# Gates of two branches as seven quarter products for eight, in a stage of their own ahead of retention

## The chip, the cores and the metric

The kernel runs on one core of a Trainium2 chip. The metric is the device time of one execution in microseconds. The core has a matrix engine (TensorE, PE in the profile; its weight loads are PEld), VectorE (DVE), ScalarE (ACT), GpSimd (POOL) and a sync engine (SP) that issues most of the DMAs. Each engine works through its own instructions in the order in which they were written out, and waits where an operand isn't there.

## The reference

Two blocks follow each other on x of 1024 tokens x 1024 columns, all in fp32. The change touches the first, a layer with four attention branches (a: NSA, b: banded, c: stick-breaking, d: retention) whose results are gated and summed:

```
h = rms_norm(x, norm_g) * (1.0 + scale) + shift
...
branches = ((y_a, a_z), (y_b, b_z), (y_c, c_z), (y_d, d_z))
for i, (y, z) in enumerate(branches):
    yi = y.reshape(B, S, BRANCH_W) * jax.nn.silu(z)
    term = jax.nn.sigmoid(h @ w_merge[i]) * (yi @ w_br[i])
    merged = term if merged is None else merged + term
return x + gate * (merged @ w_out)
```

w_merge[i] is 1024 x 1024, w_br[i] 256 x 1024. The second block (a mixer with attention, convolutions and pooling, then a feed-forward part) follows and is untouched.

## The kernel before

An fp32 product is made of three matmuls of rounded parts: each operand is split into a high part (`copy`, on ScalarE, VectorE or GpSimd) and the rest (`sub_lo`, line 157 on VectorE or 155 on GpSimd), and `mm3` (lines 229 to 231) adds high x high, high x rest and rest x high into one PSUM bank. `hT` holds h transposed and split: 8 chunks of 128 columns for each of two token halves. A gate of 128 columns and one half takes 8 x 3 = 24 matmuls of 128x512 (`gemm_T`); all gates of a branch take 8 x 2 x 24 = 384. With w_br it is 2 x 3 = 6 for each of the 16 pieces.

The branches run in the order d, a, c, b. `branch_d` projects q and k for both halves, then v, and runs retention in eight chunks. `branch_a` (its tile in `tile_of`) runs 16 tiles: two pairs of heads, eight tiles of 128 tokens each. A tile opens with the scores of the compressed keys (lines 1034 and 1035), goes on with scores of selected and window keys (s banks, lines 797 and 799), softmax on VectorE and ScalarE (lines 838 to 860), transposes of P through t banks (line 276), their split (`PT`, lines 147 and 157) and the products with v into an o bank (lines 816 and 1066).

Between those steps `fill` puts filler work, matmuls into mm banks, at places that the tables FD, FA, FB, FC give by (pair, tile): `q` a projection, `g` one group of `pre`, `m` one group of `merge`, `z` a gate of y. `pre` computes gates of 256 columns ahead and stores tanh of them to `pre_d` in DRAM, for the branches and groups of PREO (branches 0, 2, 1; six groups get used). `merge(bi, y, step)` makes four groups of 256 columns: where `pre_d` has no gate it loads w_merge and makes it, 96 matmuls; then 24 matmuls with w_br; then (1 + tanh) x product on VectorE (line 1147 for step 0, 1149 for others) and an addition to the stored sum on GpSimd (line 1150). merge(3) belongs to branch d and runs inside branch a (`mmm` at tile 3, `m` at tile 7 of the first pair). merge(1) runs last, after branch b, and its sums go split into `gT`, which the product with w_out reads.

The program is handed to a list scheduler, which writes each engine's order by priorities and estimated durations; so a piece that is shorter or sits elsewhere also moves what follows it. Matmuls of a bank wait until the bank's last reader is done; weights go through nine `w` slots and blocks of 4 KB a partition through 31 `blk` slots.

In the second block's feed-forward part the same scheme of quarter products as in the change is in use: `product` (lines 1674 to 1676) adds 12 matmuls of a quarter product into a bank, and banks are read and added to again.

Of the kernel before, what the change touches and what calls it, by code (L numbers as in the profile page):

```python
# [17 lines left out]
P = 128  # L18
# [9 lines left out]
_T = dict(STA='s', XN1=0, PWT=1, PO='0x1', PO2={}, PS=2, PSX=0, PSE='a', PB=99, PEA=(0, 1, 4), WB=8, XL=3, CLO='v', STE=None, STW=None, ST1='b', ST2='b', PLP='pvv', WLO2='v', QXP=1, LW='vp', LEAD=10, FD={0: 'g', 1: 'b', 6: 'g'}, FW=(0, 2), AG=0, PREO=(0, 2, 1), PMB=0, PWB=1, PM=3, SG=2, FA={(0, 2): 'g', (0, 3): 'mmm', (0, 7): 'qm', (1, 0): 'gg', (1, 6): 'gz'}, FB={(0, 3): 'm', (0, 7): 'qm', (1, 3): 'm', (1, 5): 'z', (1, 7): 'm'}, FC={(0, 3): 'mm', (0, 7): 'q', (1, 3): 'zm', (1, 6): 'm'}, NORM='v', NORM2='v', CS=4, CSB=8, MM=2, SB=2, TB=3, OB=1, WHI='aaav', WLO='pv', PTH='a', NW=9, NBLK=31, PTB=2, XN=1, AS=(2, 4, 6, 7), CPP=2, CALT=1, WORK='s0 A A A A A A A A p s1 q t c B c B c B c B c 0a 1a P w 5 4 6 7 g 2 3a e u c B e c B c e B c c e B 1b 0b 3b', KS=(2, 0, 3, 1))  # L28
# [48 lines left out]
def hybrid_then_mix_kernel(ctx: ExitStack, tc, I, c1, c2, out, dbg=None, upto=99):  # L77
# [306 lines left out]
    def x_norm(half):  # L384
# [9 lines left out]
        for kp in range(4):  # L394
            xT[half, kp] = blk(F32, (P, 2, 512))
            if half:
                hT.alloc(half, kp)
            for j in range(2):
# [234 lines left out]


# [20 lines left out]
    def branch_d():  # L655
        qT, kT = [blk(), blk()], [blk(), blk()]
        for half in range(2):
            if half:
                if not _T["XN1"]:
                    x_norm(1)  # L660
                start.close()
                cur[0] = att1.enter_context(tc.tile_pool(name="att1", bufs=1))
                if _T["AG"] == 0:
                    ada_gate()
            cs = slice(half * 512, (half + 1) * 512)
            for q in range(4):
# [3 lines left out]
                if q < 2:  # L670
                    copy(qT[q][:, cs], b[:], "a", QS)
                else:
                    copy(kT[q - 2][:, cs], b[:], "v")
        w = load_w([(w_in[:, :, 3212:3468], 0), (w_in[:, :, 640:652], 256)], 268, per=2)
# [4 lines left out]
        ve.tensor_scalar(g2, g2, 0.5, 0.5, op0=ALU.mult, op1=ALU.add)  # L679
        const_group(2176, ("dm", "xi", "zeta"))  # L680
        if _T["AG"] == 1:
            ada_gate()
# [477 lines left out]

    gate = main.tile([P, 8, 12], F32, name="agate", tag="agate", bufs=1)
# [27 lines left out]
    merge(1, yb, 3)  # L1189
    fill(4)  # L1190
# [475 lines left out]
    def chunks(hi, lo):  # L1666

        return lambda k: (hi[k // 2][:, k % 2, :], lo[k // 2][:, k % 2, :])
# [435 lines left out]
```

## Time and profile before

| | us |
|---|---|
| median of 3 runs (lowest, highest) | 2337.06 (2331.92, 2338.48) |
| the profiled execution, its span | 2339.66, 2337.8 |
| TensorE busy, 11004 matmuls | 2239.1 (96%) |
| VectorE busy | 1519.8 (65%) |
| ScalarE busy | 963.0 (41%) |
| GpSimd busy | 491.1 (21%) |
| granted TensorE clock, mean | 0.988 |

The times lie 6.6 us apart, 0.28%. Busy time of an engine is the time in which at least one of its instructions runs. Matmuls overlap, so their durations add up to more than the time they take; spacing of starts is what one costs. A stretch is read by comparing the busy times of the engines in it with its length.

### The profile page before, as it was taken

The page shows a single profiled execution, that of the slowest core. Times are in us where ns is not written, and L with a number is a line of the kernel's source. Part 1 is how long each engine was busy: PE and PEld are TensorE (multiplying, and loading weights), DVE is VectorE, ACT ScalarE, POOL GpSimd, SP SyncE. Part 2 cuts the span into 40 slices and gives each one's busy share as a digit, 9 for nine tenths or more (in the row PEclk, how much of TensorE's full clock was granted, in tenths as well). Part 3 has the DMA queues.
Part 4 walks back from the last instruction along what each step waited for, and adds up shares of the span by engine and source line. Part 5 has one row for each costly group of instructions (what it writes and reads, how often), then busy time and mean ns, then how long its engine had stood idle before and what let it go on. Part 6 is the DMA issues. An engine that isn't in the chain of part 4 may idle for free.

```text
span 2337.8 us, 30294 instructions
## 1 busy us (share of the span) xinstructions
PE 2239.1 (96%) x11004; PEld 1854.8 (79%) x11004; DVE 1519.8 (65%) x2952; ACT 963.0 (41%) x1937; POOL 491.1 (21%) x411
## 2 busy tenths in 40 slices
PE   8999999999988999999998998999999999999898
PEld 6788888888877778877887876777888878888787
DVE  7634456665677865634479777756666776677773
ACT  6211344444545544422322344534544453344442
POOL 4222100010265622234320000012143430000021
PEclk9999999999999999999999999999999999999999
DMA  9421221122132343224221210156556595534222
GB/s 326 156 92 62 59 68 55 46 86 68 41 102 79 109 132 94 83 80 153 90 73 36 64 59 28 56 179 205 169 182 191 194 360 193 173 108 157 94 75 90
DMA packets 202783, 272.72 MB, mean 117 GB/s; under 512 B 17086, under 2 KB 126214, under 8 KB 202634
## 3 DMA queue, kind: packets, MB, share of 16 engines
q1 hardware_dynamic: 194240, 257.95, 34.1%
q10 hardware_dynamic: 8394, 12.84, 1.7%
q8 instruction: 87, 1.43, 0.3%
q14 instruction: 62, 0.51, 0.1%
HBM read 199.43 MB, written 71.32 MB: 116 GB/s over the span
## 4 chain that ended last, share of the span: by engine, by line
PE 46%; DVE 6%; DMA 2%; ACT 1%; issue 1%; POOL 0%; SPq 0%; DVEq 0%; POOLq 0%; ACTq 0%
PE mm L230 6%; PE mm L231 6%; PE mm L229 6%; DVE blk L1334 2%; PE s L1674 2%; PE s L1676 2%; PE s L1675 2%; PE t L276 1%; PE t L2014 1%; PE t L2015 1%; PE t L2016 1%; PE s L2015 1%; PE mm L2015 1%; PE s L2016 1%; PE mm L2016 1%; PE t L1674 1%
## 5 line engine op out<-in xcount | busy, mean ns | idle before, releaser
L229 PE MATMUL mm<-blk,wh 128*128 128x512 f32 x1264 | 505.1, 400 | 16.3 <-DVE tz L1149 7.0
L230 PE MATMUL mm<-blk,wh 128*128 128x512 f32 x1264 | 501.1, 396 | 0.9 <-DVE blk L157 0.9
L231 PE MATMUL mm<-blk,wl 128*128 128x512 f32 x1264 | 499.9, 396 | 1.9 <-POOL wl L155 1.5
L229 PEld LDWEIGHTS mm<-blk,wh 128*128 128x128 f32 x1264 | 238.6, 189 | 68.5 <-DVE tz L1149 9.8
L231 PEld LDWEIGHTS mm<-blk,wl 128*128 128x128 f32 x1264 | 238.6, 189 | 52.0 <-POOL wl L155 1.9
L230 PEld LDWEIGHTS mm<-blk,wh 128*128 128x128 f32 x1264 | 238.7, 189 | 47.5 <-DVE blk L157 1.3
L155 POOL TENSOR_TENSOR wl<-wr,wh 128x1024 fp32r<-128x1024 f32 (+1 forms) x50 | 122.6, 2453 | 479.7 <-ACT wh L147 281.3
L229 PE MATMUL mm<-wh,blk 128*128 128x512 f32 (+3 forms) x544 | 197.3, 364 | 6.2 <-DVE wh L149 1.8
L231 PE MATMUL mm<-wh,blk 128*128 128x512 f32 (+3 forms) x544 | 194.9, 360 | 1.0 <-DVE blk L157 1.0
L157 DVE SCALAR_TENSOR_TENSOR wh<-blk,wh 128x1024 fp32r<-128x1024 f32 x116 | 138.5, 1222 | 72.0 <-issue 56.4
L147 ACT ACTIVATE wh<-blk 128x1024 fp32r<-128x1024 f32 x116 | 116.9, 1053 | 163.1 <-PE s L2015 77.2
L230 PE MATMUL mm<-wl,blk 128*128 128x512 f32 (+3 forms) x480 | 171.1, 357 | 9.5 <-DVE wl L157 9.1
L147 ACT ACTIVATE blk<-mm 64x512 fp32r<-64x512 f32 (+3 forms) x138 | 77.9, 570 | 172.6 <-PE mm L231 112.6
L147 ACT ACTIVATE PT<-t 128x512 fp32r<-128x512 f32 (+3 forms) x224 | 96.0, 460 | 117.4 <-PE o L816 65.0
L157 DVE SCALAR_TENSOR_TENSOR PT<-t,PT 128x512 fp32r<-128x512 f32 (+3 forms) x224 | 110.9, 515 | 38.0 <-ACT PT L147 37.2
L147 ACT ACTIVATE wh<-wr 128x1024 fp32r<-128x1024 f32 (+2 forms) x91 | 93.7, 1031 | 99.4 <-DMA wr<-in_w_in_dram 22.5
L309 POOL TENSOR_TENSOR sm<-sm,mhalf 128x1 f32<-128x1 f32 x64 | 38.0, 597 | 444.3 <-DVE sm L308 428.6
L229 PEld LDWEIGHTS mm<-wh,blk 128*128 128x128 f32 x544 | 104.1, 192 | 24.5 <-DVE wh L149 2.6
L231 PEld LDWEIGHTS mm<-wh,blk 128*128 128x128 f32 x544 | 104.1, 192 | 16.9 <-DVE blk L157 1.8
L230 PEld LDWEIGHTS mm<-wl,blk 128*128 128x128 f32 x480 | 92.3, 192 | 24.2 <-DVE wl L157 11.3
L157 DVE SCALAR_TENSOR_TENSOR wl<-wr,wh 128x1024 fp32r<-128x1024 f32 (+2 forms) x69 | 88.2, 1279 | 30.8 <-PE mm L230 14.0
L1150 POOL TENSOR_TENSOR acc<-tz,acc 128x512 f32<-128x512 f32 x48 | 68.8, 1436 | 132.0 <-DVE tz L1149 91.4
(364 smaller groups left out, 4857.1 us busy)
## 6 DMA issues: line engine op xcount, KB each, us to landing
acc<-acc SPq DMA_DIRECT2D x96, 256.0 KB, 2.7
wr<-in_w_merge_dram SPq DMA_DIRECT2D x32, 512.0 KB, 3.6
wu<-in_w_up_dram SPq DMA_DIRECT2D x32, 512.0 KB, 5.1
blk<-in_w_down_dram SPq DMA_DIRECT2D x32, 512.0 KB, 6.9
blk<-ss SPq DMA_DIRECT2D x32, 512.0 KB, 4.7
wr<-in_w_in_dram SPq DMA_DIRECT2D x27, 512.0 KB, 4.4
ss<-us SPq DMA_DIRECT2D x48, 256.0 KB, 2.2
blk<-sa SPq DMA_DIRECT2D x24, 512.0 KB, 3.4
```

The lines of the kernel that those rows point to most:

```text
L147: return ac.activation(dst, src, AF.Copy, scale=1.0 if scale is None else scale)
L155: po.tensor_tensor(lo, x, hi.bitcast(F32), op=ALU.subtract)
L157: ve.scalar_tensor_tensor(out=lo, in0=x, scalar=scale, in1=hi.bitcast(F32), op0=ALU.mult, op1=ALU.subtract)
L229: pe.matmul(dst, sh, mh, start=(i == 0), stop=False)
L230: pe.matmul(dst, sh, ml, start=False, stop=False)
L231: last = pe.matmul(dst, sl, mh, start=False, stop=(i == n - 1))
L1150: po.tensor_tensor(acc[:], t[:], acc[:], op=ALU.add)
L1334: ve.scalar_tensor_tensor(out=acc[:, c:c1], in0=u[:, c - l:c1 - l], scalar=w, in1=acc[:, c:c1], op0=ALU.mult, op1=ALU.add)
L1674: pe.matmul(dst, wh, xh, start=first and k == 0, stop=False, skip_group_check=True)
L1675: pe.matmul(dst, wh, xl, start=False, stop=False, skip_group_check=True)
L2015: pe.matmul(d, sh[:, c, ts_], tl[:, c, :], start=False, stop=False)
L2016: last = pe.matmul(d, sl[:, c, ts_], th[:, c, :], start=False, stop=stop)
```

## The change

Gates of branches 3 and 1 (GS) leave merge and are made by `gate_group`, eight groups of 256 columns, between branch d's v projection and its retention. h and w_merge are cut in quarters (512 columns of h by 512 tokens; 512 by 128 of w), and a 2 x 2 product of quarters is put together from seven products of sums instead of eight products (the Strassen-Winograd scheme): 7 x 12 = 84 matmuls of 128x512 a group for 96. `gate_sums` makes the four sums of h's quarters (12 additions of 128x1024 on VectorE), `gate_parts` splits them (8 copies on ScalarE, 8 splits on VectorE). A group makes four sums of w's quarters, splits them, and reads and reuses three banks (mm, s, t). The results are stored to `pre_d`, 32 transfers of 256 KB.

The unsplit second half of x (`xT[1]`) is kept in the `wada` tiles, q and k are stored to DRAM (`qk_d`, four of 512 KB) and loaded again before retention, and `ada_gate` (16 VectorE instructions, eight loads of 512 KB) runs behind the stage. merge(3) finds its gates in `pre_d`, so that its code is unchanged but its groups hold 24 matmuls. merge(1) gives way to `merge_last`: by token halves, 16 steps of two loads of 256 KB, 6 matmuls, and three VectorE instructions and one ScalarE copy. Its matmuls are 96 as before. `chunks`, `product` and `wslot` only stand further up.

```diff
+    def gate_sums():
+        for kp in range(2):
+            b11, b21 = [(hT.h[0][q][:].bitcast(F32), hT.l[0][q][:].bitcast(F32)) for q in (kp, kp + 2)]
+            b12, b22 = xT[1, kp], xT[1, kp + 2]
+            t1, t2, t3, t4 = [blk(F32, (P, 2, 512)) for _ in range(4)]
+            ve.tensor_tensor(t1[:], b12, b11[0], op=ALU.subtract)
+            ve.tensor_tensor(t1[:], t1[:], b11[1], op=ALU.subtract)
+            ve.tensor_tensor(t3[:], b22, b12, op=ALU.subtract)
+            ve.tensor_tensor(t2[:], b22, t1[:], op=ALU.subtract)
+            ve.tensor_tensor(t4[:], b21[0], t2[:], op=ALU.subtract)
+            ve.tensor_tensor(t4[:], t4[:], b21[1], op=ALU.add)
...
+    def gate_group(b_, g):
+        rf = cur[0].tile([P, 8, 256], F32, name=nm("wu"), tag="wu", bufs=2)
+        sy.dma_start(rf[:], kview(I["w_merge"][0, b_])[:, :, g * 256:(g + 1) * 256])
...
+        ha, la = wslot((8, P)), wslot((8, P))
+        copy(ha[:], rf[:, :, :P], "a")
+        sub_lo(la[:], rf[:, :, :P], ha[:])
+        f23, f14 = wslot((2, 4, P), F32), wslot((2, 4, P), F32)
+        ve.tensor_tensor(f14[:, 0], a21, a22, op=ALU.add)
+        ve.tensor_tensor(f23[:, 0], f14[:, 0], a11, op=ALU.subtract)
+        ve.tensor_tensor(f23[:, 1], a11, a21, op=ALU.subtract)
+        ve.tensor_tensor(f14[:, 1], a12, f23[:, 0], op=ALU.subtract)
+        h23, s23 = wslot((2, 4, P)), wslot((2, 4, P))
+        copy(h23[:], f23[:], "a")
+        sub_lo(s23[:], f23[:], h23[:])
...
+        a = mmb()
+        product(a[:], lambda k: (ha[:, k], la[:, k]), gate_right("b11"), True)
+        copy(va[:, 0], a[:], "a")
+        product(a[:], lambda k: (ha[:, 4 + k], la[:, 4 + k]), gate_right("b21"), False)
+        done(va[:, 1], a[:], 0, 0)
+        b, c = stb(), trb()
+        product(b[:], lambda k: (h23[:, 0, k], s23[:, 0, k]), gate_right("t2"), True)
+        ve.tensor_tensor(ub[:, 0], b[:], va[:, 0], op=ALU.add)
+        product(b[:], lambda k: (h23[:, 1, k], s23[:, 1, k]), gate_right("t3"), False)
+        ve.tensor_tensor(ub[:, 1], b[:], va[:, 0], op=ALU.add)
+        product(c[:], lambda k: (h14[:, 0, k], s14[:, 0, k]), gate_right("t1"), True)
+        ve.tensor_tensor(ub[:, 1], c[:], ub[:, 1], op=ALU.add)
+        done(ub[:, 1], ub[:, 1], 1, 1)
...
     def branch_d():
...
-                start.close()
-                cur[0] = att1.enter_context(tc.tile_pool(name="att1", bufs=1))
-                if _T["AG"] == 0:
-                    ada_gate()
...
+        for d, t in zip(qk_d, qT + kT):
+            sy.dma_start(d[:], t[:])
+        gate_sums()
...
+        gate_parts()
         w = load_w([(w_in[:, :, 3212:3468], 0), (w_in[:, :, 640:652], 256)], 268, per=2)
...
+        for b_ in _T["GS"]:
+            for g in range(4):
+                gate_group(b_, g)
...
+        for d, t in zip(qk_d, qT + kT):
+            sy.dma_start(t[:], d[:])
         const_group(2176, ("dm", "xi", "zeta"))
+        if _T["AG"] == 0:
+            ada_gate()
...
+    def merge_last(bi, y, step):
...
+        for half in range(2):
+            for k in range(KC):
+                ta = blk(F32, (P, 2, 512))
+                t, acc = ta[:, 0], ta[:, 1]
+                sy.dma_start(acc, acc_d[step - 1][k][half][:])
+                sy.dma_start(t, pre_d[bi, k, half][:])
+                bp = mmb()
+                gemm_T(bp[:], wbr[k // 4], k % 4 * P, y, half)
+                ve.scalar_tensor_tensor(out=t, in0=t, scalar=1.0, in1=bp[:], op0=ALU.add, op1=ALU.mult)
+                ve.tensor_tensor(acc, t, acc, op=ALU.add)
+                if k % 2 == 0:
+                    gT.alloc(half, k // 2)
+                copy(gT.hi(k, half), acc, "a", 0.5)
+                sub_lo(gT.lo(k, half), acc, gT.hi(k, half), "v", 0.5)
...
-    merge(1, yb, 3)
-    fill(4)
+    merge_last(1, yb, 3)
```

Two places in the orders. In the rows mm is a filler's bank, s, t and o are banks of scores, transposes and products with v; lines of the changed kernel lie some 119 higher in branch a (916 and 918 for 797 and 799, 935 for 816, 1185 for 1066).

The first is TensorE in branch a, first pair, at the scores of tile 6 and the products of tile 5. Before:

```order
L799 MATMUL s_3925<-blk_2264,blk_2421 128x512
L230 MATMUL mm_3425<-blk_682,wh_3376 128x512
L231 MATMUL mm_3425<-blk_681,wl_3377 128x512
L797 MATMUL s_3929<-blk_2263,blk_2421 128x128
L799 MATMUL s_3929<-blk_2264,blk_2421 128x128
L229 MATMUL mm_3425<-blk_681,wh_3376 128x512
L816 MATMUL o_3696<-PT_3804,blk_2398 128x256 x3
L816 MATMUL o_3696<-PT_3804,blk_2399 128x256
L816 MATMUL o_3696<-PT_3813,blk_2399 128x256
L1066 MATMUL o_3696<-cT_3715,vc 128x256
L276 MATMUL t_3830<-c_63,Pm_3728 128x128 x2
```

The same place after:

```order
L935 MATMUL o_4472<-PT_4560,blk_3510 128x256 x4
L935 MATMUL o_4472<-PT_4570,blk_3511 128x256 x2
L916 MATMUL s_4696<-blk_3375,blk_3532 128x128
L918 MATMUL s_4696<-blk_3376,blk_3532 128x128
L916 MATMUL s_4701<-blk_3375,blk_3533 128x512
L918 MATMUL s_4701<-blk_3376,blk_3533 128x512
L916 MATMUL s_4705<-blk_3375,blk_3533 128x128
L918 MATMUL s_4705<-blk_3376,blk_3533 128x128
L935 MATMUL o_4472<-PT_4580,blk_3510 128x256 x3
L935 MATMUL o_4472<-PT_4580,blk_3511 128x256
L276 MATMUL t_4606<-c_63,Pm_4504 128x128 x2
```

The matmuls into mm banks are gone from between scores, products and transposes. From the scores that open tile 5 of the first pair to those that open tile 0 of the second there is none in the changed order; from tile 2 to tile 5 there are 108 where before has 146; from the opening of the second pair's last tile to the transposes of its selected keys' P there are 23 where before has 111. In all, TensorE's order has 96 matmuls less.

The second is VectorE in the last merge (line 1149, after 1292, is the product with the gate; 1293 the addition that line 1150 did on GpSimd; 157 the split into gT or of w_out's weights). Before:

```order
L1149 SCALAR_TENSOR_TENSOR tz_9932<-tz_9932,mm_9959 128x512
L157 SCALAR_TENSOR_TENSOR blk_9927<-acc_9930,blk_9926 128x512
L1149 SCALAR_TENSOR_TENSOR tz_9972<-tz_9972,mm_9999 128x512
L157 SCALAR_TENSOR_TENSOR blk_10009<-acc_9970,blk_10008 128x512
L157 SCALAR_TENSOR_TENSOR wl_10061<-wr_10054,wh_10060 128x1024
L1149 SCALAR_TENSOR_TENSOR tz_10014<-tz_10014,mm_10041 128x512
L157 SCALAR_TENSOR_TENSOR blk_10009<-acc_10012,blk_10008 128x512
```

After:

```order
L1292 SCALAR_TENSOR_TENSOR blk_10506<-blk_10506,mm_10509 128x512
L1293 TENSOR_TENSOR blk_10506<-blk_10506 128x512
L1292 SCALAR_TENSOR_TENSOR blk_10520<-blk_10520,mm_10523 128x512
L157 SCALAR_TENSOR_TENSOR blk_10503<-blk_10506,blk_10502 128x512
L1293 TENSOR_TENSOR blk_10520<-blk_10520 128x512
L149 CAST wh_10668<-wr_10664 128x1024
L157 SCALAR_TENSOR_TENSOR blk_10533<-blk_10520,blk_10532 128x512
L1292 SCALAR_TENSOR_TENSOR blk_10536<-blk_10536,mm_10539 128x512
```

A step has three VectorE instructions instead of two, and the matmuls of a step between them are 6 (into the mm bank) instead of 30; some of w_out's weights (wr, wh) are split late among them.

## Rows read from the trace of the kernel before

**Rows 1.** Page: busy time by engine; the chain by engine; a group of section 5.

```profile
PE 2239.1 (96%) x11004; PEld 1854.8 (79%) x11004; DVE 1519.8 (65%) x2952; ACT 963.0 (41%) x1937; POOL 491.1 (21%) x411
...
PE 46%; DVE 6%; DMA 2%; ACT 1%; issue 1%; POOL 0%; SPq 0%; DVEq 0%; POOLq 0%; ACTq 0%
...
L157 DVE SCALAR_TENSOR_TENSOR wh<-blk,wh 128x1024 fp32r<-128x1024 f32 x116 | 138.5, 1222 | 72.0 <-issue 56.4
```

**Rows 2.** Stretches: length; busy us of PE, PEld, DVE, ACT, POOL; PE clock; DMA share; GB/s.

```profile
290.00:650.00 360.00, 360.00 (x1968) 310.02 (x1967) 223.34 (x712) 164.62 (x415) 41.24 (x32) 1.00 0.18 59
311.00:361.00 50.00, 50.00 (x272) 42.96 (x272) 35.53 (x124) 22.71 (x63) 2.59 (x1) 1.00 0.14 48
361.00:442.00 81.00, 81.00 (x443) 69.60 (x442) 53.73 (x157) 33.31 (x80) 7.78 (x3) 1.00 0.17 56
584.00:620.00 36.00, 36.00 (x193) 30.78 (x192) 23.63 (x67) 16.57 (x39) 8.21 (x6) 1.00 0.12 37
985.00:1095.00 110.00, 102.28 (x440) 81.97 (x439) 45.23 (x44) 27.89 (x42) 42.29 (x24) 1.00 0.36 116
1075.00:1095.00 20.00, 15.38 (x64) 11.59 (x63) 14.89 (x10) 6.41 (x9) 14.21 (x6) 1.00 0.70 240
1000.00:1020.00 20.00, 20.00 (x89) 16.43 (x88) 6.52 (x7) 4.51 (x7) 6.30 (x4) 1.00 0.10 27
1425.00:1475.00 50.00, 40.57 (x194) 29.36 (x193) 46.15 (x137) 32.00 (x76) 3.25 (x5) 0.93 0.14 43
1450.00:1500.00 50.00, 44.11 (x220) 33.99 (x221) 42.16 (x116) 30.14 (x66) 2.57 (x4) 0.97 0.11 32
1650.00:1900.00 250.00, 250.00 (x1094) 205.13 (x1093) 171.96 (x193) 119.09 (x173) 91.42 (x56) 1.00 0.64 205
1900.00:1950.00 50.00, 45.54 (x190) 36.02 (x189) 39.43 (x39) 23.20 (x30) 6.08 (x4) 0.97 0.89 328
```

**Rows 3.** Timeline of TensorE: start, duration, instruction.

```profile
999.71 0.39 PE L230 MATMUL mm<-blk,wh 128*128 128x512 f32 x1
...
1003.15 0.39 PE L230 MATMUL mm<-blk,wh 128*128 128x512 f32 x1
```

**Rows 4.** A TensorE group, 1000 to 1020: count, then busy us, mean ns.

```profile
L231 PE MATMUL mm<-blk,wl 128*128 128x512 f32 x30 | 11.8, 392 | 0.0
```

**Rows 5.** Timeline of TensorE: matmuls that open tiles of branch a.

```profile
361.34 0.18 PE L1034 MATMUL s<-kch,blk 128*128 128x32 f32 x1
...
454.05 0.23 PE L1034 MATMUL s<-kch,blk 128*128 128x32 f32 x1
```

**Rows 6.** TensorE's filler matmuls, 361 to 442.

```profile
L229 PE MATMUL mm<-blk,wh 128*128 128x512 f32 x79 | 31.5, 399 | 0.0
L231 PE MATMUL mm<-blk,wl 128*128 128x512 f32 x79 | 31.2, 395 | 0.0
L230 PE MATMUL mm<-blk,wh 128*128 128x512 f32 x78 | 30.9, 396 | 0.0
```

**Rows 7.** VectorE's groups, 361 to 442; last: idle before them, and its releaser.

```profile
L157 DVE SCALAR_TENSOR_TENSOR PT<-t,PT 128x512 fp32r<-128x512 f32 x11 | 7.6, 689 | 10.1 <-ACT PT L147 9.9
...
L157 DVE SCALAR_TENSOR_TENSOR wl<-wr,wh 128x1024 fp32r<-128x1024 f32 x3 | 3.7, 1218 | 1.0 <-PE mm L230 1.0
```

**Rows 8.** Timeline of VectorE: its first instruction of the tile opened at 454.05.

```profile
461.90 0.17 DVE L1039 CUSTOM_DVE_ANT_0 cs<-s,cst 128x32 f32<-128x32 f32 x1
```

**Rows 9.** VectorE's gate evacuations, 584 to 612.

```profile
L619 DVE SCALAR_TENSOR_TENSOR tz<-tz,mm 128x512 f32<-128x512 f32 x4 | 2.7, 682 | 0.0
```

**Rows 10.** Line 1149, 960 to 1100 (min/median/max ns), and VectorE's idle time before it.

```profile
L1149 DVE SCALAR_TENSOR_TENSOR tz<-tz,mm x16: 672/686/687, 969.2 to 1078.7; 128x512 f32<-128x512 f32 x16
...
  PE mm L231: 33.7, 12
```

**Rows 11.** One of VectorE's additions in the feed-forward stage, 1650 to 1900.

```profile
L1801 DVE TENSOR_TENSOR blk<-s,pa 128x512 f32<-128x512 f32 x15 | 10.3, 689 | 11.4 <-PE s L1676 11.4
```

**Rows 12.** Page: DMA issues, KB each, median us to landing.

```profile
blk<-in_w_down_dram SPq DMA_DIRECT2D x32, 512.0 KB, 6.9
```

More of the change, by code (lines that the diff above doesn't have):

```diff
@@ L632, in fill, with chunks, product @@
                 fillers.pop(0)()
+    def chunks(hi, lo):
+        return lambda k: (hi[k // 2][:, k % 2, :], lo[k // 2][:, k % 2, :])
+    def product(dst, w, x, first):
+        for k in range(4):
+            (wh, wl), (xh, xl) = w(k), x(k)
+            pe.matmul(dst, wh, xh, start=first and k == 0, stop=False, skip_group_check=True)
+            pe.matmul(dst, wh, xl, start=False, stop=False, skip_group_check=True)
+            last = pe.matmul(dst, wl, xh, start=False, stop=k == 3, skip_group_check=True)
+        return last
@@ new lines, in wslot @@
+    def wslot(shape, dt=F32R):
+        return main.tile([P] + list(shape), dt, name=nm("wh"), tag="w", bufs=NW)
+    gsum, gpart = {}, {}
+    def gate_sums():
[9 more added lines that the diff above has]
+            ve.tensor_tensor(t4[:], t4[:], b21[1], op=ALU.add)
+            for name, t in (("t1", t1), ("t2", t2), ("t3", t3), ("t4", t4)):
+                gsum[name, kp] = t
@@ new lines, in gate_parts, with part @@
+    def gate_parts():
+        left = [_T["GP"]]
+        def part():
+            left[0] -= 1
+            if left[0] < 0:
+                return blk(F32R, (P, 2, 512))
+            return cur[0].tile([P, 2, 512], F32R, name=nm("gt"), tag="gt", bufs=_T["GP"])
+        for name in ("t2", "t3", "t1", "t4"):
+            gpart[name] = [[], []]
+            for kp in range(2):
+                hi, lo = part(), part()
+                copy(hi[:], gsum[name, kp][:], "a")
+                sub_lo(lo[:], gsum[name, kp][:], hi[:])
+                gpart[name][0].append(hi)
+                gpart[name][1].append(lo)
@@ L1664, in hybrid_then_mix_kernel @@
              for i in ("a11", "a12", "a22", "s1", "s2", "s3", "s4")}
-    def chunks(hi, lo):
-        return lambda k: (hi[k // 2][:, k % 2, :], lo[k // 2][:, k % 2, :])
-    def product(dst, w, x, first):
-        for k in range(4):
-            (wh, wl), (xh, xl) = w(k), x(k)
-            pe.matmul(dst, wh, xh, start=first and k == 0, stop=False, skip_group_check=True)
-            pe.matmul(dst, wh, xl, start=False, stop=False, skip_group_check=True)
-            last = pe.matmul(dst, wl, xh, start=False, stop=k == 3, skip_group_check=True)
-        return last
     def t_pair(t):
@@ L1755, in hybrid_then_mix_kernel @@
     cur[0] = ph.enter_context(tc.tile_pool(name="up", bufs=1))
-    def wslot(shape, dt=F32R):
-        return main.tile([P] + list(shape), dt, name=nm("wh"), tag="w", bufs=NW)
     def us_tile():
```

44 lines of the change are left out of this document (39 added, 5 removed).

## The prediction

> **What bounds the kernel now.** I read the page first: TensorE is busy for 96% of the span and carries 46% of the chain that ended last, VectorE 6% [rows 1]. So TensorE sets the end. But its busy time is no price list: its matmuls overlap. In a stretch that does nothing else, 89 matmuls of 128x512, of about 392 ns each, fill 20 us [rows 2, 4], and the starts of neighbours lie (1003.15 - 999.71)/15 = 0.229 us apart [rows 3]. A matmul added or taken away is worth 0.229 us as long as TensorE has the next one ready.
>
> Second, the table by stretch shows where that holds. Branch a (290 to 650 us) keeps TensorE busy for 360 of 360 us with VectorE at 223 us, 62%; the second block's feed-forward stage is just as dense, 250 of 250 us, with VectorE at 69%. The second block's attention (1425 to 1475) has few matmuls to fill with: VectorE is busy for 46.15 of 50 us there, TensorE for 40.57; its granted clock of 0.93 there is a mean of its two levels, 2.4 GHz for most of the time and 1.2 for the rest [rows 2]. Softmax attention without fillers is thus VectorE's work, at 92% of its time (84% in the neighbouring stretch, 42.16 of 50 us); with fillers it is TensorE's.
>
> **What it removes.** Eight groups of 96 gate matmuls become eight of 84: 96 fewer, 96 x 0.229 = 22.0 us of TensorE. This is saved only where TensorE stays full.
>
> **What it moves: hole 1, in branch a.** merge(3) was branch a's filler. Each of its groups held 96 gate and 24 w_br matmuls; now it holds 24. The orders show what that leaves. Between the compressed-score matmuls that open tile 5 of the first head pair (tiles count from 0) and tile 0 of the second pair, 361 to 442 us in the trace of before [rows 2, 5], there are 79 + 79 + 78 = 236 filler matmuls [rows 6]; the changed order has none in the same stretch. TensorE's own need is 81.0 - 236 x 0.229 = 27 us. VectorE is busy for 53.73 us there [rows 2]. Three splits of w_merge (3.7 us [rows 7]) leave; nothing else does, since softmax and the accumulation of merge(3) stay: 50 us. At 92% that takes 54 us, so 54 - 27 = 27 us are lost. The bounds: in before VectorE starts the tile that TensorE opened at 454.05 only at 461.90 [rows 5, 8], so some of its work trails into stretches that still have fillers; that and 100% use give 50 - 27 - 8 = 15 us. At the 84% of the other unfilled stretch it would be 60 - 27 = 33. I take 24, near the 92% row, since it is the same softmax code, less 3 us for the trailing. Tiles 2 to 4 (311 to 361) keep most of their fillers, 38 fewer (8.7 us): TensorE 41.3 us against VectorE 35.5 [rows 2], nothing lost.
>
> One rule of the Trainium skill speaks against this move. Perfetto Trace Analysis, section Optimization Strategy, says that where the most contended engine changes over time, interleaving those regimes may improve performance; the change takes an interleaving apart. The filled and the unfilled attention of this trace agree with it (62% and 92% of VectorE, above). By it the gates would be better left where they were; counted by matmuls alone, the forecast would be 2337 - 22 = 2315 us.
>
> **Hole 2, the end of branch a.** Fillers that followed are used up sooner, so the last tile of the second pair has 23 fillers where before has 111, 88 fewer, 20.2 us. That stretch is 584 to 620: TensorE 36 - 20.2 = 15.8 us, VectorE 23.6 us, 2.7 us of which are four gate evacuations that went with them [rows 2, 9]; (23.6 - 2.7)/0.92 = 23. Lost: 7; bounds 0 (VectorE's work trails into branch c) and 10 (all 23.6 us at 92%). I take 6.
>
> **The last merge.** Before, merge(1) has 480 matmuls, 110 us by 0.229, and 985 to 1095 is nearly all its own, with VectorE idle before the 16 accumulations for 33.7 us waiting for TensorE [rows 10]; TensorE loses 110 - 102.3 = 7.7 us there, at the end, when w_out has to come and the last sums pass through POOL [rows 2]. After, a step is 6 matmuls, 1.37 us, and three VectorE instructions of 128x512 (the second addition comes over from POOL): 3 x 0.686 = 2.06 us [rows 10]. Sixteen steps: 33 us of VectorE on 22 us of TensorE, 11 us lost. The first half's steps are interleaved with branch b's last tiles, which need VectorE too, so this isn't hidden by them. Against it stands what is left of the 7.7 us: w_out products of the first half need no late sum. Net between 11 - 7.7 = 3 and 11; and 0 if the final steps hide behind the output product. I take 6.
>
> **The stage itself and its ends.** Seven quarter products a group, four of them accumulated into a bank that VectorE or ScalarE has just read, are what the feed-forward stage does, and TensorE misses nothing there; VectorE waits for TensorE before its additions (11.4 us ahead of one kind) [rows 2, 11]. Cost 0. At its start VectorE has 12 additions and 8 splits of 128x1024 at about 1.22 us [rows 1], 24 us, next to 96 q and k matmuls (22 us) and the v projection; they are covered if they start in time. At its end qT and kT return by four transfers of 512 KB; the slowest loads of that size take 6.9 us [rows 12], and the order leaves some 60 matmuls (14 us) behind which they can land. ada_gate's 16 VectorE instructions and eight loads move behind the stage, into a part with an idle VectorE. The 32 stores of gates queue on SP ahead of the weights of later groups; no reader wants the stored gates before branch a, but a late group can wait for its weights. Bounds 0 and 8 us (one exposed load, or a third of the additions uncovered); I take 2. The clock at 0.93 in unfilled stretches costs nothing where VectorE is the bound; it is in these bounds.
>
> **Sum.** -22 + 24 + 6 + 6 + 2 = +16. The profiled execution took 2339.7 us (span 2337.8), 2.6 above the median 2337.1. On the median: 2353 us. Own range of this case: lows 15 + 0 + 3 + 0 - 22 = -4 (2333), highs 33 + 10 + 11 + 8 - 22 = +40 (2377); the ends won't all come together, so 2338 to 2372.
>
> **Rivals.**
> (a) Faster: VectorE's work trails away from the holes. It is 62% busy in branch a as a whole; if the first hole's last third is worked off under the fillers behind it, its price is 54 - 18 - 27 = 9 us, the second and the tail give 0, and the start 0 to 2: -22 + 9 + 1 = -12, 2325 us. For it: VectorE's lag of 8 us in before, and that TensorE's order, not VectorE's, is what counts. Against it: in the hole score banks, transposes and products alternate on TensorE in order, each for VectorE's result, and VectorE itself waits 9.9 us for ScalarE's copies of P [rows 7], so it can't run at 100%. It decides from the point where less than 36 of its 50 us fall into the hole.
> (b) No change: the hole costs its lower bound, 15, and the rest 7: 2337 us.
> (c) The last merge is bound by loads. 32 x 256 KB and 8 x 512 KB of w_out are 12.6 MB; at the 240 GB/s of 1075 to 1095 that is 52 us for 33 us of work, less what is loaded ahead, at the 328 GB/s of 1900 to 1950 it is 38 [rows 2]. 5 to 19 us more than the sum: 2365. For it: one SP queue carries both and w_out stands behind. Against it: free blocks let loads run ahead under branch b.
> (d) The stage stalls at each of its 32 hand-overs between reading and accumulating, about 1 us each (one 0.69 us addition and its start): +32, 2385. Against it: the feed-forward rows.
> That the change doesn't do what it says is no rival: the order has 96 matmuls less.
>
> **Chances.** A measurement can tell 0.3%, 7 us, from no change: below 2330, 2330 to 2344, above. My forecast with its spread 0.46 (all but 0.02 of it slower), (a) 0.18, (b) 0.17, (c) 0.12, (d) 0.07. Slower 0.44 + 0.12 + 0.07 = 0.63; same 0.17 + 0.02 + 0.01 of (a) = 0.20; faster 0.17. The range leaves out the faster half of (a) and (d): 2322 to 2376.
>
> **What would show it.** Right: in branch a a stretch of some 50 us in which TensorE is busy for about half and VectorE for nine tenths, with score and product banks waiting for VectorE; a shorter one before branch c; about 154 us for the 672 gate matmuls without a gap; merge_last in 33 us or more. Wrong: the hole's VectorE share under 80%, its tiles 5 to 7 taking under 45 us; or matmuls of the gate stage waiting for VectorE.

## The result and the profile after

The changed kernel takes 2400.68 us at the median of four runs (2396.11 to 2406.07), the kernel before 2334.78 in the four runs beside it (2331.92 to 2338.48): a ratio of 1.0279, with an interval of 1.0256 to 1.0302. It is slower by 66 us where 16 were forecast, and lies outside the range. The profiled execution took 2398.94 us, of which the span is 2397.2; its mean granted clock is 0.972, against 0.988 before.

The page of the changed kernel, to be read against [rows 1]:

```profile
PE 2255.8 (94%) x10908; PEld 1860.9 (78%) x10908; DVE 1600.9 (67%) x3080; ACT 992.7 (41%) x1973; POOL 450.2 (19%) x387
...
PE 43%; DVE 6%; DMA 2%; ACT 1%; issue 1%; POOL 0%; SPq 0%; DVEq 0%; POOLq 0%; ACTq 0%
...
L229 PE MATMUL mm<-blk,wh 128*128 128x512 f32 x1008 | 411.3, 408 | 36.3 <-DVE blk L1292 17.8
```

There are 96 matmuls less, as forecast, and TensorE's busy time is nevertheless 17 us longer. One reason is that where the clock is low, a matmul lasts 0.63 or 0.79 us and not 0.39 (timeline below). The last row says where its longest waits are: 17.8 us before first matmuls of a product, for line 1292, VectorE's product with the gate in merge_last.

The time goes by stretches. The marks are instructions that both kernels have; branch a's are in these two answers for the matmuls that open its tiles (before, then after; they run from the first to the last of 16 tiles):

```profile
L1034 PE MATMUL s<-kch,blk x32: 177/262/263, 278.2 to 584.3; 128*128 128x32 f32 x32
```

```profile
L1153 PE MATMUL s<-kch,blk x32: 177/262/394, 455.8 to 720.0; 128*128 128x32 f32 x32
```

"Change" below is the change of a stretch's length less 0.229 us [rows 3] for each 128x512 matmul that it holds more, so what TensorE loses there over before. The counts are from the traces, and the other matmuls are the same in both kernels.

| stretch | us before, after | 128x512 matmuls | change | forecast |
|---|---|---|---|---|
| start to branch a's first tile | 278.2, 455.8 | 772, 1444 | +23.8 | +2 |
| to its last tile | 306.1, 264.2 | 1012, 725 | +23.8 | +24 |
| to branch c's first scan on VectorE | 45.7, 31.6 | 154, 64 | +6.4 | +6 |
| to the last softmax with sinks of branch b | 344.5, 342.6 | 988, 954 | +6.0 | 0 |
| to w_out's first matmul | 104.0, 43.5 | 430, 73 | +21.3 | +6 |
| to the end | 1259.3, 1259.5 | 4664, 4664 | +0.1 | 0 |

The sum is +81.4; less 96 x 0.229 = 22.0 it is the 59.4 us by which the spans of the two profiled executions differ (the medians differ by 65.9). That is so by the way the column is made. That the saving is there is shown by the gate stage below, where 672 matmuls take the place of 768 and TensorE waits for next to nothing. The two holes cost what was forecast, and two terms failed: the stage with its ends (23.8 for 2), and the last merge with branch b's last tiles (27.3 for 6).

Some stretches of after: length; busy us of PE, PEld, DVE, ACT, POOL; granted clock; DMA share; GB/s:

```profile
95.00:128.00 33.00, 26.68 (x141) 22.76 (x140) 26.86 (x27) 11.81 (x15) 5.12 (x3) 0.90 0.44 145
128.00:300.00 172.00, 170.36 (x785) 140.01 (x784) 83.55 (x118) 52.73 (x73) 2.40 (x1) 1.00 0.30 107
...
400.00:425.00 25.00, 19.33 (x103) 15.43 (x103) 11.07 (x41) 6.53 (x11) 5.38 (x6) 0.86 0.33 82
525.00:575.00 50.00, 39.46 (x231) 32.35 (x229) 41.82 (x160) 30.10 (x79) 0.00 (x0) 0.91 0.04 11
529.00:571.20 42.20, 33.95 (x197) 27.39 (x196) 36.30 (x145) 25.53 (x70) 0.00 (x0) 0.92 0.05 13
720.00:751.60 31.60, 27.51 (x159) 23.51 (x158) 21.41 (x66) 17.13 (x40) 2.27 (x4) 0.95 0.00 1
...
1100.00:1125.00 25.00, 13.33 (x48) 9.58 (x49) 16.09 (x27) 5.58 (x10) 1.28 (x1) 0.80 0.53 189
```

The second row is the gate stage: TensorE misses 1.6 of 172 us, and of its 672 gate matmuls nearly all start 0.23 or 0.24 us after the one before. The first is the sums ahead of it: VectorE works 26.86 of 33 us, in 27 instructions of which many take over 1.2 us, and TensorE has time over. The third is the end of retention, in which no engine is full: TensorE waits for VectorE there (below). The fourth is hole 1 in branch a, with VectorE at 84%; the fifth is its tiles 5 to 7 alone, and the sixth hole 2. The last is merge_last, where TensorE has work for little more than half.

TensorE's waits at the end of retention (engine, line, what it waited for: us, times, longest), 395 to 425, for a normalized result (line 863) and for the reading of a bank of branch a's first projection (1087):

```profile
PE t L276 <- DVE Pm L863: 3.0, 1, 3.0
PE mm L229 <- DVE blk L1087: 2.7, 1, 2.7
```

The waits in merge_last, 1075 to 1150:

```profile
ACT blk L147 <- DVE blk L1293: 34.1, 14, 9.5
...
PE mm L229 <- DVE blk L1292: 17.8, 6, 9.0
DVE blk L1292 <- DMA blk<-pre: 11.1, 4, 7.3
```

Read from below: VectorE's product waits for the gate's load, TensorE for a bank that this product has not read yet. The longest of these waits in the timelines of TensorE, VectorE and SP's queue (start, duration, instruction, idle time before it):

```profile
1109.20 0.40 PE L231 MATMUL mm<-blk,wl 128*128 128x512 f32 x1
1118.57 0.79 PE L229 MATMUL mm<-blk,wh 128*128 128x512 f32 x1 [8.97 <-DVE blk L1292]
1119.16 0.63 PE L230 MATMUL mm<-blk,wh 128*128 128x512 f32 x1
1119.59 0.63 PE L231 MATMUL mm<-blk,wl 128*128 128x512 f32 x1
...
1122.56 0.40 PE L229 MATMUL mm<-blk,wh 128*128 128x512 f32 x1
```

```profile
1117.83 0.69 DVE L1292 SCALAR_TENSOR_TENSOR blk<-blk,mm 128x512 f32<-128x512 f32 x1 [7.34 <-DMA blk<-pre]
```

```profile
1092.63 0.32 SPq L1289 DMA_DIRECT2D blk<-pre  x1
1106.77 0.81 SPq L1400 DMA_DIRECT2D xt<-in_x_dram  x2
1107.63 0.43 SPq L1288 DMA_DIRECT2D blk<-acc  x1
1108.10 0.65 SPq L1289 DMA_DIRECT2D blk<-pre  x1
```

SP issues no load from 1092.6 to 1106.8. At the head of its queue stands a load of x (line 1400, for the sum behind w_out); the sums and gates stand behind it. It waited for its buffer: in turn for the last work of branch b on TensorE, ScalarE and GpSimd (9.0, 2.6 and 2.1 us). Of SP's waits (1080 to 1140):

```profile
SPq L194 <- POOL wl L155: 11.4, 1, 11.4
SPq L1400 <- PE o L935: 9.0, 1, 9.0
SPq L194 <- PE mm L231: 7.3, 1, 7.3
...
SPq L1400 <- ACT ju L147: 2.6, 1, 2.6
SPq L1400 <- POOL blk L622: 2.1, 1, 2.1
```

Line 194 loads weights: loads of w_out do the same from 1072.5 to 1085.4 and from 1117.6 to 1124.7.

The queue is not all of it. The gate for which VectorE waits until 1117.8 is issued at 1108.10 and lands at 1117.73, 9.6 us later, where the median of the 256 KB loads of `pre_d` into tz is 3.2 us. The stretches before and after the issue:

```profile
1098.00:1106.80 8.80, 5.26 (x23) 3.78 (x24) 8.19 (x17) 2.75 (x8) 1.28 (x1) 1.00 0.01 2
1106.80:1118.00 11.20, 2.55 (x10) 1.43 (x9) 3.76 (x7) 1.85 (x3) 0.00 (x0) 0.75 0.92 322
```

While the queue stands, the DMA engines have nothing to do (0.01). Then two loads of x and three vectors from ScalarE's queue, 512 KB each, are issued within 1.1 us, all ahead of the gate, and the DMA engines are at 0.92. With the sum and the gate these are 3.1 MB, which at 322 GB/s take 9.8 us (an estimate). So the mean of 0.53 over 25 us hides an idle stretch and a full one.

### The profile page after: what moved, and what is told of

Same layout as the page of the kernel before. It is cut to its first block, busy times and chain, and to the rows that moved or that the text cites. A ratio compares the mean times of both kernels' runs of the same rounds, so it can differ in the third digit from the quotient of the medians.

```text
span 2397.2 us, 30350 instructions
## 1 busy us (share of the span) xinstructions
PE 2255.8 (94%) x10908; PEld 1860.9 (78%) x10908; DVE 1600.9 (67%) x3080; ACT 992.7 (41%) x1973; POOL 450.2 (19%) x387
## 4 chain that ended last, share of the span: by engine, by line
PE 43%; DVE 6%; DMA 2%; ACT 1%; issue 1%; POOL 0%; SPq 0%; DVEq 0%; POOLq 0%; ACTq 0%
PE mm L229 6%; PE mm L230 6%; PE mm L231 5%; DVE blk L1471 3%; PE s L644 2%; PE s L646 2%; PE s L645 2%; PE t L276 1%; PE t L2135 1%; PE t L2136 1%; PE t L2137 1%; PE s L2136 1%; PE mm L2136 1%; PE s L2137 1%; PE t L644 1%; PE t L646 1%
## 5 line engine op out<-in xcount | busy, mean ns | idle before, releaser
L229 PE MATMUL mm<-blk,wh 128*128 128x512 f32 x1008 | 411.3, 408 | 36.3 <-DVE blk L1292 17.8
L231 PE MATMUL mm<-blk,wl 128*128 128x512 f32 x1008 | 404.2, 401 | 0.3 <-DVE wl L157 0.3
L230 PE MATMUL mm<-blk,wh 128*128 128x512 f32 x1008 | 402.7, 400 | 0.4 <-POOL blk L155 0.4
L229 PEld LDWEIGHTS mm<-blk,wh 128*128 128x128 f32 x1008 | 193.9, 192 | 82.8 <-DVE blk L1292 20.3
L231 PEld LDWEIGHTS mm<-blk,wl 128*128 128x128 f32 x1008 | 193.1, 192 | 41.2 <-DVE wl L157 0.8
L230 PEld LDWEIGHTS mm<-blk,wh 128*128 128x128 f32 x1008 | 193.6, 192 | 37.9 <-POOL blk L155 0.9
L155 POOL TENSOR_TENSOR wl<-wr,wh 128x1024 fp32r<-128x1024 f32 (+1 forms) x42 | 102.4, 2440 | 621.8 <-ACT wh L147 469.6
L147 ACT ACTIVATE wh<-wr 128x1024 fp32r<-128x1024 f32 (+2 forms) x79 | 80.9, 1025 | 85.7 <-PE mm L231 21.6
L935 PE MATMUL o<-PT,blk 128*128 128x256 f32 x508 | 92.6, 301 | 14.2 <-DVE PT L157 13.8
L276 PE MATMUL t<-c,Pm 128*128 128x128 f32 x508 | 86.2, 289 | 17.7 <-DVE Pm L150 10.1
```

What stands on the lines that cost most here:

```text
L147: return ac.activation(dst, src, AF.Copy, scale=1.0 if scale is None else scale)
L155: po.tensor_tensor(lo, x, hi.bitcast(F32), op=ALU.subtract)
L229: pe.matmul(dst, sh, mh, start=(i == 0), stop=False)
L230: pe.matmul(dst, sh, ml, start=False, stop=False)
L231: last = pe.matmul(dst, sl, mh, start=False, stop=(i == n - 1))
L276: pe.transpose(dst, src, ident)
```

## The experiments

Each is a change of the changed kernel unless said otherwise. "Lost over before" is the last-but-one column of the table above.

**Gates of branch 1 alone in the stage.** merge(3) gets its own gates back.

```diff
-GS=(3, 1)
+GS=(1,)
```

> The stage makes branch 1's gates only (four groups, 336 matmuls); branch 3's gates go back into merge(3) as fillers of branch a. 48 matmuls fewer than before, 48 more than after. Theory H (the holes are where the time went): branch a is full again, so 30 us of the loss go; 2400.7 + 11 - 30 = 2382. Theory P (the sum of the prediction is right but for the holes' size): everything lost is in the holes, so 2334.8 - 11 + 6 + 2 = 2332. A full branch a with about 2382 says that some 45 us are lost elsewhere: at the last merge and between the stage and branch a.

Measured: 2371.81 us, ratio 1.0149 (1.0128 to 1.0171). Branch a and its end lose 0.0 us over before, with all 1012 and 154 matmuls back; the start still loses 18.7 and the end (last two rows with a change) 3.1 + 23.6. So holes 1 and 2 are the missing gate matmuls and nothing else, half the groups in the stage cost nearly as much at the start as all of them, and the last merge's loss has nothing to do with branch a.

**Gates of branch 3 alone in the stage**, with the old merge(1) and its gates.

```diff
-GS=(3, 1)
+GS=(3,)
...
-    merge_last(1, yb, 3)
+    merge(1, yb, 3)
+    fill(4)
```

> The stage makes branch 3's gates only, and the last merge is the one of before with branch 1's gates made in it, 384 matmuls between its steps. 48 matmuls more than after. If the last merge lost its time because its gate matmuls, which covered its loads, are gone: its 28 us go, 2400.7 + 11 - 28 = 2384. The holes of branch a stay (30 us), and what is lost from the stage to branch a stays about as with four groups (some 19 us). Theory V or a cause in the new code alone would be fixed here as well, so this run tells only what branch 1's part costs in all.

Measured: 2380.68 us, ratio 1.0194 (1.0166 to 1.0222). Lost over before: start 24.8, branch a and its end 24.9 + 5.1, last merge -1.8 - 0.2. This is the mirror of the first: the last merge's loss goes when its gates come back. In its last merge TensorE is full again, and VectorE idle for most of the time:

```profile
1070.00:1095.00 25.00, 24.56 (x107) 20.20 (x108) 6.90 (x9) 5.21 (x8) 7.95 (x6) 1.00 0.24 72
```

**The old last merge with stored gates.** All gates in the stage, but merge(1) instead of merge_last.

```diff
-    merge_last(1, yb, 3)
+    merge(1, yb, 3)
+    fill(4)
```

> The last merge is the one of before (by groups, second addition on GpSimd), with the gates that the stage stored. Theory V (VectorE's third instruction bounds the last merge): a step is back at two VectorE instructions, 11 us go, 2390. Theory Q (loads of the last merge stand on SP behind loads of x and of w_out that wait): x's loads no longer stand among them, so TensorE's two long stalls, 9.0 and 4.9 us, go, and with the additions 14 to 23 us: 2378 to 2387. If the old merge's few acc and tz buffers bind in turn, no change: 2400.

Measured: 2411.11 us, ratio 1.0326 (1.0292 to 1.0359). It loses 5.1 + 27.4 at the end, more than merge_last. Neither the order by halves nor the addition on VectorE is the cause, then: a last merge without gate matmuls loses some 30 us in either form.

**Loads of sums and gates issued by ScalarE.**

```diff
-                sy.dma_start(acc, acc_d[step - 1][k][half][:])
-                sy.dma_start(t, pre_d[bi, k, half][:])
+                ac.dma_start(acc, acc_d[step - 1][k][half][:])
+                ac.dma_start(t, pre_d[bi, k, half][:])
```

> As the changed kernel, but the 32 loads of the last merge (stored sums and gates) are issued by ScalarE's queue in place of SP's; the arithmetic and its order by engine are the same. Theory Q (queue): the loads no longer stand behind the waiting loads of x and w_out; the stalls of 9.0 and 4.9 us before the product with the gate go, 2400.7 - 14 = 2387. Theory V (VectorE): nothing changes but noise, 2400, and ScalarE gains 32 issues.

Measured: 2410.09 us, ratio 1.0315 (1.0294 to 1.0335), slower than after. The waits of 1075 to 1150:

```profile
ACT blk L147 <- DVE blk L1293: 39.8, 13, 6.3
...
PE mm L229 <- DVE blk L1292: 22.9, 8, 5.8
DVE blk L1292 <- DMA blk<-pre: 17.9, 10, 4.1
```

The loads no longer stand behind x, but behind ScalarE's copies, which wait for VectorE's additions, which wait for the loads. That moved the wait; it neither showed nor refuted that loads are the cause, which took the next one.

**One sum and one gate loaded once**, and used in all 16 steps, so that 30 of 32 loads are left out.

```diff
+        one = blk(F32, (P, 2, 512))
+        sy.dma_start(one[:, 1], acc_d[step - 1][0][0][:])
+        sy.dma_start(one[:, 0], pre_d[bi, 0, 0][:])
...
-                sy.dma_start(acc, acc_d[step - 1][k][half][:])
-                sy.dma_start(t, pre_d[bi, k, half][:])
```

> As the changed kernel, but the last merge loads one stored sum and one stored gate and uses these two for all 16 steps (the other 30 loads are left out, and with them the right values of the last merge). Engine work is the same, three VectorE instructions a step. Theory L (the last merge waits for its loads): the waits of VectorE for the loaded gates, 11 us, and TensorE's stalls of 9.0 and 4.9 us go, and what stays is VectorE's rate: some 14 to 20 us less, 2380 to 2387. Theory V (VectorE's 3 x 0.69 us a step against 1.37 us of matmuls): 2400, at most 5 less.

Measured: 2388.51 us, ratio 1.0223 (1.0196 to 1.0249): 12 us less than after. The end loses 4.1 + 11.1 = 15.2 over before, where after loses 27.3. So 12 of these are the loads of sums and gates, and 15 are not. TensorE's waits, 1080 to 1140:

```profile
PE mm L229 <- DVE blk L1293: 6.2, 6, 1.6
PE mm L229 <- ACT blk L147: 4.4, 1, 4.4
```

The first row is the bank that the product with the gate (1293 here) still has to read. The second, the longest wait, is ScalarE's copy of branch b's last result, behind GpSimd's product with its z gate: not a step of merge_last, but the end of branch b, which has nothing beside it.

**The same, with the second addition on GpSimd**, as in the kernel before: two VectorE instructions a step instead of three.

```diff
-                ve.tensor_tensor(acc, t, one[:, 1], op=ALU.add)
+                po.tensor_tensor(acc, t, one[:, 1], op=ALU.add)
```

> As e7_loads_once (30 of the 32 loads of the last merge left out, and its right values with them), with the second addition on GpSimd again. Theory V for what e7 left, some 19 us between branch b's end and w_out: a VectorE step falls from 2.06 to 1.37 us, as long as TensorE's, 11 us go, 2388 - 11 = 2377. If the rest is the chain of one step (product, VectorE, GpSimd 1.3 us, ScalarE, VectorE) over few buffers, it gets longer: 2388 to 2395.

Measured: 2388.27 us, ratio 1.0219 (1.0196 to 1.0241), and 2.9 + 12.3 = 15.2 us lost at the end: no change. The addition takes 1.29 us on GpSimd and 0.69 on VectorE, so a step's chain grew while VectorE's work shrank, and the two could cancel; but with VectorE at 68% its rate, which the prediction made its term from, is not the bound. Its stretch in the last merge:

```profile
1100.00:1125.00 25.00, 16.21 (x61) 11.22 (x60) 17.11 (x30) 8.27 (x19) 10.94 (x9) 0.86 0.44 139
```

No engine is at three quarters of the time. With loads out of the way, what is left is a step's chain (6 matmuls, product, addition, copy, split) and the end of branch b, both without gate matmuls to run beside them, and a granted clock of 0.86. How much of the 15 us each of the three makes is open.

**The start: the v projection behind the stage**, away from the sums.

```diff
+        for d, t in zip(qk_d, qT + kT):
+            sy.dma_start(t[:], d[:])
+        w = load_w([(w_in[:, :, 3212:3468], 0), (w_in[:, :, 640:652], 256)], 268, per=2)
```

> The v projection (192 matmuls of 128x268) moves from ahead of the stage to behind it, beside retention, where before had it. Theory R (retention lost its cover: 13 us between the stage and branch a): its matmuls fill retention again, 2400.7 - 13 = 2388, and TensorE's stalls at the end of retention, 3.0 and 2.7 us, go. Theory B (the loss at the stage's start is VectorE's burst of additions in front of the v projection's copies): the 4.7 us wait for the copy goes but TensorE has only 96 q and k matmuls over 24 us of additions: between 2394 and 2406. If neither is a cause of weight, 2400.

Measured: 2397.44 us, ratio 1.0264 (1.0244 to 1.0285); the start loses 25.2. No gain: where the v projection stands does not matter.

**The start taken apart.** Three kernels have the gates inside merge(3) and merge(1) as in the kernel before (GS=(), the old last merge), so that of the changed start there is only: q and k stored and loaded again and ada_gate moved; the same with the sums of h made and split, and not used; and ada_gate moved alone. The first and the third also leave out the sums, the third the four stores and loads of q and k as well:

```diff
-GS=(3, 1)
+GS=()
...
-        gate_sums()
...
-        gate_parts()
```

> The kernel before (no gate groups, merge(1) at the end) with the moves around the stage alone: q and k stored to DRAM and loaded again before retention, ada_gate behind the v projection, pools in the new order; no sums, no parts. In the order of TensorE retention starts behind the v projection here, and in the middle of the q and k projection in before. Theory S (storing and reloading q and k takes retention away from the projections that covered it): the 13 us that retention loses appear without any gate group, 2335 + 13 = 2348. Theory G (the stage's groups cause it, by their stores and loads on SP or their banks): 2335 to 2338.

> As e11_spill_only, with the sums and parts of h computed and not used (12 additions, 8 copies and 8 splits of 128x1024). Theory S and the burst of VectorE work (7 us at the stage's start): 2348 + 7 = 2355. If the burst is hidden behind the projections, the same as e11_spill_only.

> As e11_spill_only without the store and the reload: only ada_gate and the pools are moved. Theory S: retention overlaps with the projections again, 2335 to 2338. If moving ada_gate's 16 VectorE instructions and 8 loads behind the v projection is the cause, it is as slow as e11_spill_only.

Measured: 2341.30, 2347.39 and 2347.38 us; ratios 1.0016 (1.0006 to 1.0026), 1.0043 (1.0028 to 1.0058) and 1.0044 (1.0026 to 1.0062). Storing and loading q and k costs little (0.2 us lost at the start in the trace, which is of the fastest of ten executions; 4 us by the medians). The sums cost 6 us by the medians, 8.3 by the spans of the profiled executions; to branch a's first tile the trace shows 11.0. The first row is the first kernel, the second the one with sums, at the same place:

```profile
100.00:125.00 25.00, 25.00 (x175) 23.58 (x174) 3.61 (x10) 2.46 (x5) 1.35 (x1) 1.00 0.54 191
```

```profile
100.00:125.00 25.00, 18.95 (x102) 16.48 (x101) 21.80 (x26) 9.50 (x11) 1.40 (x1) 0.90 0.57 191
```

With the sums VectorE is at 21.80 of 25 us, and TensorE, which needs its results, falls from 25.00 to 18.95. The third missed its expectation: without storing q and k it is slower by 6 us, and loses 11.5 at the start, though it does less. A difference of this size thus comes about without any work added; the likely reason is the order that the scheduler writes, which was not shown. Of the 11.5 us, 10.5 lie behind retention's first matmul. ada_gate's 16 instructions stand there, from 128.6 to 150.9; but in the first kernel they stand beside retention too, from 131.8 to 150.5, and cost nothing. So the price of the sums may hang on the order around them too.

**ada_gate ahead of the groups**, so that it does not stand beside retention.

```diff
+        if _T["AG"] == 0:
+            ada_gate()
         for b_ in _T["GS"]:
             for g in range(4):
                 gate_group(b_, g)
```

> As the changed kernel, with ada_gate (16 VectorE instructions, eight loads of 512 KB) issued ahead of the gate groups and not behind them. Theory A (at the stage's end ada_gate's loads and the reload of q and k queue on SP with the stores of gates, and retention's fillers come late: TensorE loses 6.5 us between 325 and 350): the loss goes there, 2400.7 - 6 = 2394, unless the stage itself now waits. If retention's losses come from the lack of matmuls beside it: 2400.

Measured: 2392.16 us, ratio 1.0243 (1.0223 to 1.0263), an interval that overlaps that of after. In its trace the start loses 23.6, as after: from retention's first matmul on 7.0 less, ahead of it 6.8 more. But this trace is of the slowest of its four executions (2398.63 us; the others took 2389.10 to 2392.20), so whether the 7 us come back ahead of retention is open. The median is where the expectation had it.

**A group of gates more as filler in retention's last chunk.**

```diff
-FD={0: 'g', 1: 'b', 6: 'g'}
+FD={0: 'g', 1: 'b', 6: 'g', 7: 'g'}
```

> As the changed kernel, with one more group of stored gates (branch 2, 96 matmuls) as filler behind retention's last chunk; it leaves merge(2) in branch b. Theory R (from retention's end to branch a TensorE runs out of fillers and loses 7.5 us): these go, 2393, if branch b can spare the group. If nothing is gained there, or branch b loses as much, 2400.

Measured: 2406.21 us, ratio 1.0299 (1.0278 to 1.0321). The start loses 13.3 instead of 23.8; but the 96 matmuls are missing in branches c and b, which lose 27.7 instead of 6.0.

**Two groups of gates more as fillers in branch a's hole.**

```diff
-(0, 3): 'mmm', (0, 7): 'qm',
+(0, 3): 'mmm', (0, 4): 'g', (0, 5): 'g', (0, 7): 'qm',
```

> As the changed kernel, with two more groups of stored gates (branch 2, 192 matmuls, 44 us) as fillers at tiles 4 and 5 of branch a's first pair, in the hole; they leave merge(2) in branch b. Theory H (the hole is 27 us of TensorE on 50 us of VectorE): its loss of 24 us goes, and branch b, which loses nothing in before, gives up two groups: between 2377 and 2390. If the hole's price were a chain of waits and not missing matmuls, the fillers would only lengthen it: 2400 or more.

Measured: 2411.5 us, ratio 1.0312 (1.0285 to 1.0339). Branch a loses 10.0 instead of 23.8, branches c and b 34.6 instead of 6.0. The fillers fill the hole; and there are no others for the place that they are taken from.

**Normalization of branch a's P partly on ScalarE**, to take work off VectorE in the hole.

```diff
-                               nsl, hd, weight=gw(1))
+                               nsl, hd, weight=gw(1), norm='va')
```

> As the changed kernel, but in branch a every second normalization of P is made by ScalarE in place of VectorE (some 7 us of VectorE's 50 in the hole). Theory H (the hole is bound by VectorE's throughput): the hole gets shorter by some 7 us, 2393, and the second one by 1 to 2. If it is bound by the chain from scores over softmax to the products, moving an instruction of the same length to another engine changes nothing: 2400.

Measured: 2396.77 us, ratio 1.0259 (1.0243 to 1.0274). Branch a loses 21.0 instead of 23.8 and its end 3.8 instead of 6.4; the hole with the tile ahead of it (tiles 4 to 7) shortens from 66.2 to 61.9 us.

```profile
525.00:575.00 50.00, 40.56 (x245) 31.98 (x244) 40.45 (x161) 35.56 (x85) 0.00 (x0) 0.98 0.04 11
```

VectorE's share is 81% now and the hole still there: its rate can be no more than a part of the bound, the chain of scores, softmax and products the rest. The granted clock is 0.98 here and was 0.91, so part of the gain may be the clock's; the two were not taken apart.

## Why the prediction was wrong, point by point

**What bounds the kernel, and the saving.** Right. 96 matmuls less are 22.0 us less wherever TensorE is full, and in the stage, where the seven products stand, it is.

**Holes 1 and 2.** Right in cause and size: 23.8 and 6.4 measured for 24 and 6, and 0.0 when the gates return (gates of branch 1 alone in the stage). But not as the prediction drew it. Tiles 5 to 7 of the first pair took 42.1 us, under the 45 that it named as a sign against itself: they lose 14.7 us, the next pair's tile 0 loses 5.5, and the other tiles 3.6 together, 2.3 of them in tiles 2 to 4, for which the prediction had nothing. So VectorE's work trails into the next tile, as rival (a) had it: 36.3 of its 50 us fall into the hole, next to the 36 at which the prediction let (a) decide. But that tile has ten 128x512 matmuls fewer than before (22 for 32), and loses too. And VectorE is at 84 to 86%, near the bound that stood for the 33, not at 92%; TensorE is busy for 39.46 of 50 us, not for half. Two errors of the step met, more trailing and a lower share of VectorE, so that the size came out right in part by luck. In hole 2 VectorE is busy for 21.41 of 31.6 us, 68%: there too the size was right and the share was not.

**The last merge: the term that failed, 27.3 for 6.** The step counted rates: three VectorE instructions against six matmuls, less what TensorE lost in before. Taking one of the three away changed nothing (the addition on GpSimd). What it left out is that the 24 gate matmuls of a step were cover for its latencies. 12 us are loads: rival (c), for which 5 to 19 us were worked out. It was right in kind and size, and in part in its mechanism. Bandwidth, from which it was priced, is one part: the DMA engines are at 0.92 while the longest wait lasts. The other part it named in a clause only ("one SP queue carries both"): SP's queue held a load of x that waited for its buffer, so the DMA engines stood idle for 8.8 us first. The argument against it ("free blocks let loads run ahead") was true until 1092.6 us, and no longer. The other 15 us remain with one sum and one gate for all steps: the chain of a step, the end of branch b and the clock, in shares that stay open; 11 was the highest that the step allowed. Rival (c)'s 2365 stood on a sum whose other terms were too low.

**The stage and its ends: the other term that failed, 23.8 for 2.** Its middle was right, 1.6 us idle in 172, and rival (d) fell: of the 32 hand-overs three show a wait, 1.6 us in all. Its ends were not. Against the kernel that only stores q and k, after loses 14.5 us more ahead of retention's first matmul (79.8 against 65.3, each less 0.229 for each 128x512 matmul) and 9.0 from there to branch a (45.3 against 36.3). Of the first, the sums explain up to 11, by that kernel with sums (76.1 against 65.3). One trace stands behind each; in the seven kernels whose code is that of after up to branch a, the first figure lies between 78.3 and 83.7 and the second between 45.3 and 45.9. The prediction saw their 24 us of VectorE (27.6 in the trace of after) and wrote "covered if they start in time"; they are not, for TensorE's next work, the v projection, comes out through VectorE and ScalarE, whose copies queue behind them:

```profile
PE mm L229 <- DVE agate L149: 4.7, 1, 4.7
...
ACT gt L147 <- DVE blk L663: 8.9, 1, 8.9
```

(waits of after, 95 to 128; line 149 copies a result of the projection, line 663 is one of the sums.) Yet moving the projection gained nothing, so this wait is where the burst shows and not by itself the cause. Of the second, 9.0 us, what is shown is that a filler group there takes 10.5 away, and that 7.0 go when ada_gate doesn't stand beside it. Matmuls are not missing by count: from retention's first one to branch a there are 482 of 128x512 against 484, of which the stage's last 24 come at its start. The prediction took "a part with an idle VectorE" for a place where work is free; in retention TensorE waits for short VectorE steps (3.0 and 2.7 us at its end). Its terms for storing q and k were right, at about nothing. How the remaining 4 us ahead of retention come about, and why the kernel without storing q and k is slow, stays open: it would take the order itself held fixed, which was not tried.

**The rule on interleaving** (the Trainium skill, Perfetto Trace Analysis, section Optimization Strategy) was weighed for branch a alone, where the traces agree with it: 84% of VectorE and 79% of TensorE without fillers, both under 100, and TensorE full with them. Matmuls to run beside a wait were missed at two more places, retention and the last merge, at which the prediction did not ask; there no engine is full (77% of TensorE at most in the row of retention, 64% of VectorE in that of the last merge).

**The chances.** Slower had 0.63. The size is outside the range since two terms went beyond their upper bounds, by 16 each (23.8 against 8, 27.3 against 11); all four terms at those bounds gave 2377.

## What to carry to other kernels

Before independent matmuls are removed or gathered into a dense stage, ask at every place that they leave what they covered, loads and short chains as well as a busy engine; in this kernel each of three places lost 24 to 30 us, more than the 22 us that the whole change saves. Moving the remaining ones only moves the hole (two experiments), because there are no more to be had. Price an exposed step by its chain, by when its loads are issued and by what is issued with them, not by the mean rates of its engines: with no engine at three quarters of its time, it may still be what TensorE waits for.

## What the runs showed of the hardware

Not expected was how dear a stall is behind itself. After the 8.97 us wait the matmuls start 0.43 us apart for 3 us, from 1119.16 (above), where they start 0.229 apart else; from 1118.57 to 1122.56 nine starts take 4.0 us and not 2.1. The granted clock is at the lower of its two levels, 1.2 GHz, and its mean is 0.80 in that stretch, and 0.86 at 400 to 425 in retention, where the longest wait of TensorE was 3.0 us. The prediction held that the clock costs nothing where VectorE is the bound; where TensorE had to catch up after this wait, it cost these 2 us.

A load waiting for its buffer at the head of SP's queue kept all loads behind it from being issued, for some 13, 14 and 7 us; the DMA engines' share was 0.01 in the last 8.8 us of the second. What had gathered then came at once: 0.92 and 322 GB/s for 11.2 us, and 256 KB took 9.6 us to land. Issuing them on ScalarE's queue put them behind ScalarE's waiting copies instead, and was no better.
